# Token tile 0 of the second block first, tile 1 behind its first gathers, and float32 query products

## The chip, the cores and the metric

One core of one Trainium2 chip. The metric is the time of the whole program on the device in microseconds (us); the time of a kernel is the median of its runs. TensorE is called PE here, VectorE DVE, ScalarE ACT, GpSimd POOL and SyncE SP.

## The reference

256 tokens of 1024 channels pass two layers of a first block (three kinds of attention, an output product, a layer norm) and one layer of a second block. The change concerns the second block alone:

```python
h = rmsnorm(x, norm1_g) * (1 + sc1) + sh1
q, k, v, u = split(h @ w_in)                       # 512 channels each
attn = dilated_attention(q, k, v)                  # 8 heads of 64, causal
pool = multiscale_pool(u, pool_w, pool_scale)
x = x + g1 * (concat([attn, pool]) @ w_out)
h2 = rmsnorm(x, norm2_g) * (1 + sc2) + sh2
x = x + g2 * peer_ffn(h2, peer_wq, peer_subkeys, peer_u, peer_v)
out = rmsnorm(x, final_g)

def peer_ffn(x, w_q, sub_keys, expert_u, expert_v):    # 8 heads, q: 2 x 128 each
    s = einsum('chpk,pnk->chpn', x @ w_q, sub_keys)    # scores of 2 x 128 sub-keys
    sv, si = top_k(s, 16)                              # of each half
    top_v, top_pos = top_k(all 16 x 16 sums of sv, 16)
    eid = si[0] * 128 + si[1] at top_pos               # 16 of 16384 experts
    gate = softmax(top_v)
    act = gelu(einsum('cd,chkd->chk', x, expert_u[eid]))
    return einsum('chk,chkd->cd', gate * act, expert_v[eid])
```

## The kernel before

The tokens are two tiles of 128 (tile 0, tile 1), one token for each partition. Weights come in the order of the program through SP's queue, half a megabyte at a time (`raw`); `split` (lines 154 to 164) rounds each into a high part on ACT (`wh`, L159) and a rest on DVE (`wl`, L160), and `mm3` (L213 to L215) makes of each float32 product three quick ones: high by high, high by rest, rest by high.

**Second block** (`block2`, lines 971 to 1052). Queries and keys, values, then the pooling half are projected for both tiles. Meanwhile the dilated attention runs as a task beside the projections, piece by piece (`dilated`, `attend`): a piece is two heads of one tile, scores on PE, bias and maximum on DVE, exponentials on ACT, transposes and the product with the values on PE. The output product follows, first the pooling half of the channels, then the attention half (`y`, transposed), each for both tiles; then residual, norm (`normed`) and the transposed, scaled and shifted norm for both tiles (`affine_transposed`). `warm` puts dummy matmuls ahead of what follows.

**Experts** (`peer`, lines 1110 to 1213). For each of 8 heads the query product of both tiles (`feature`, three quick products of 128x256 for each weight tile), its copy `q`, the scores against the sub-keys (L1150) and their copy `sc`. Behind head 0 the route of (head 0, tile 0) is worked out on DVE (`route`: top 16 of each half, top 16 of their sums, the experts' numbers `eid`). The other 15 routes run later as tasks on DVE beside the rows. A route gives 16 experts for each of 128 tokens; a gather (L1165, an indirect DMA issued by POOL) brings for one of the 16 the rows `u` and `v` of all 128 tokens, 8 KB for each. That makes 16 routes x 16 = 256 gathers; the arrived tile is called a row below. DVE takes the product of `u` with the token's state, summed (L1199), ACT the gelu (L1202), DVE the gate (L1203); ACT makes a diagonal matrix `d` of the result (L1207), and PE adds `d` times `v` to the output sum in two halves of 512 channels (L1209). When PE is through with a row, its place in the buffer (`SLOTS`, 12 of 1 MB) is free for the next gather. Dot products, gelus and sums go in groups of four rows. Behind 128 rows `last` ends a tile: residual (L1174, L1175), norm, output.

Within an engine the order of the list is what the scheduler of the language makes of the program's text and of priorities; a query product stands ahead of a row's sum where its place in the text is earlier. POOL issues its gathers strictly in the order of its list.

Of the kernel before, what the change touches and what calls it, by code (L numbers as in the profile page):

```python
# [31 lines left out]
WARM = (27, 50, 25)  # L32
PACE = 0.55
SLOTS = 12
# [111 lines left out]
class Prog:  # L146
# [467 lines left out]
    def layer(self, l, x, xt, mem):  # L614
# [109 lines left out]
        for tt in range(2):  # L724
# [17 lines left out]
            if l + 1 == NL:  # L742
                self.normed(x, tt, ss[tt], self.xn)
# [186 lines left out]
    def normed(self, x, tt, ss, xn):  # L930

        nc = self.nc
        nc.vector.tensor_tensor(ss[:, 2:3], ss[:, 0:1], ss[:, 1:2], op=OP.add)
        self.rstd(ss[:, 2:3], ss[:, 2:3], 1.0 / D, self.eps6)
        self.hold = nc.vector.tensor_scalar(xn[:, tt, :512], x[:, tt, :512], ss[:, 2:3], None, op0=OP.mult)
        nc.scalar.activation(xn[:, tt, 512:], x[:, tt, 512:], AF.Copy, scale=ss[:, 2:3])

    def dilated(self, heads, qT, kT, v, y):
# [6 lines left out]
        def bias(s, ps, heads, tt):  # L945
            c = slice(128, 384) if tt else slice(0, 128)
            self.behind(nc.vector.tensor_tensor(s, ps, self.alibi[:, heads[0]:heads[1] + 1:2, c], op=OP.add))
# [23 lines left out]
    def block2(self, x, bp):  # L971
# [3 lines left out]
        self.h2 = self.xtp = bp  # L975
# [8 lines left out]
        self.alibi = bp.tile([128, 8, 384], F, name="alibi")  # L984
        qT = bp.tile([128, 4, S], F, name="q2")
        kT = bp.tile([128, 4, S], F, name="k2")
        v = bp.tile([128, 2, 512], F, name="v2")
        u = bp.tile([128, 2, 512], F, name="u2")
        y = bp.tile([128, 2, 512], F, name="y2")
# [13 lines left out]
        for h in range(8):  # L1003
            self.behind(nc.vector.scalar_tensor_tensor(self.alibi[:, h, :], dist, -float(2.0 ** -(h + 1)), lcnt, op0=OP.mult, op1=OP.add))
# [6 lines left out]
        self.pooling(u, band, wp, yp, bp)  # L1011
        g1 = self.mod[2]
        po = [[self.pacc.tile([128, 512], F, name="bank") for _ in range(2)] for _ in range(2)]

        def product(yt, first, tt, cg, j, w):
            for k in range(2):
                self.mm3(po[tt][cg], [t[:, 2 * j + k, tt * 128:(tt + 1) * 128] for t in yt],
# [260 lines left out]
```

## Time and profile before

| | us |
|---|---|
| median of 3 runs | 1453.67 (1451.47 to 1454.97) |
| the profiled execution | 1449.26 |
| its span, first to last instruction | 1447.5 |
| PE busy | 1263.4 (87%) |
| DVE busy | 1015.0 (70%) |
| ACT busy | 593.6 (41%) |
| POOL busy | 244.0 (17%) |
| all DMA | 405.30 MB, mean 280 GB/s |
| of these the gathers | 268.45 MB, 44.8% of 16 engines' span |

The profiled execution is one run, 4.4 us below the median of the three; durations are read from it alone. Shares of busy time are means over a program of very different stages, so the stages have to be read one by one. All tables of the trace count from the start of the span.

### The profile page before, as it was taken

The page shows a single profiled execution, that of the slowest core. Times are in us where ns is not written, and L with a number is a line of the kernel's source. Part 1 is how long each engine was busy: PE and PEld are TensorE (multiplying, and loading weights), DVE is VectorE, ACT ScalarE, POOL GpSimd, SP SyncE. Part 2 cuts the span into 40 slices and gives each one's busy share as a digit, 9 for nine tenths or more (in the row PEclk, how much of TensorE's full clock was granted, in tenths as well). Part 3 has the DMA queues.
Part 4 walks back from the last instruction along what each step waited for, and adds up shares of the span by engine and source line. Part 5 has one row for each costly group of instructions (what it writes and reads, how often), then busy time and mean ns, then how long its engine had stood idle before and what let it go on. Part 6 is the DMA issues. An engine that isn't in the chain of part 4 may idle for free.

```text
span 1447.5 us, 17295 instructions
## 1 busy us (share of the span) xinstructions
PE 1263.4 (87%) x5798; PEld 868.2 (60%) x5798; DVE 1015.0 (70%) x2044; ACT 593.6 (41%) x1290; POOL 244.0 (17%) x260
## 2 busy tenths in 40 slices
PE   8999999988999999989988987777787777878786
PEld 7888897767898988778777633233333332333332
DVE  6488888667589886667576677777775977755554
ACT  5567667445567665434443322222222322221112
POOL 0000000000000000000003243343333334333330
PEclk9999999999999999999998999998999899999898
DMA  8464365676563444466439799999999899999994
GB/s 303 128 221 135 115 200 168 191 222 215 168 194 98 153 146 127 166 220 200 154 115 398 300 422 421 421 422 421 421 421 422 352 421 422 421 422 421 421 421 191
DMA packets 74536, 405.30 MB, mean 280 GB/s; under 512 B 8912, under 2 KB 9296, under 8 KB 40784
## 3 DMA queue, kind: packets, MB, share of 16 engines
q0 software_dynamic: 36864, 268.45, 44.8%
q1 hardware_dynamic: 37584, 135.75, 28.5%
q8 instruction: 46, 0.75, 0.2%
q14 instruction: 42, 0.34, 0.1%
HBM read 403.12 MB, written 1.05 MB: 279 GB/s over the span
## 4 chain that ended last, share of the span: by engine, by line
PE 45%; DMA 37%; DVE 9%; ACT 4%; issue 4%; POOL 0%; DVEq 0%; ACTq 0%; POOLq 0%; SPq 0%
DMA uv<-in_puv_dram,eid 31%; PE bank L214 8%; PE bank L213 8%; PE bank L215 8%; PE acc L1209 8%; DMA raw<-in_wu_dram 6%; PE bank L371 2%; ACT wh L159 2%; DVE uv L1199 2%; DVE wl L160 2%; PE bank L461 2%; PE bank L221 1%; PE bank L510 1%; PE bank L437 1%; PE bank L549 1%
## 5 line engine op out<-in xcount | busy, mean ns | idle before, releaser
L1209 PE MATMUL acc<-uv,d 128*128 128x512 f32 x1024 | 495.2, 641 | 129.2 <-ACT d L1207 129.2
L1209 PEld LDWEIGHTS acc<-uv,d 128*128 128x128 f32 x1024 | 204.8, 205 | 414.7 <-issue 239.8
L1199 DVE CUSTOM_DVE_ANT_0 uv<-hid,uv 128x1024 f32<-128x1024 f32 x256 | 313.2, 1223 | 183.0 <-DMA uv<-in_puv_dram,eid 171.9
L1165 POOL DMA_INDIRECT uv<-in_puv_dram,eid x256 | 243.8, 952 | 1167.6 <-DVE eid L1104 761.0
L160 DVE TENSOR_TENSOR wl<-raw,wh 128x1024 fp32r<-128x1024 f32 (+1 forms) x184 | 223.2, 1214 | 122.0 <-ACT wh L159 121.6
L159 ACT ACTIVATE wh<-raw 128x1024 fp32r<-128x1024 f32 (+1 forms) x184 | 192.8, 1050 | 203.8 <-DMA raw<-in_wu_dram 92.4
L1202 ACT ACTIVATE dot<-dot 128x4 f32<-128x4 f32 (+1 forms) x66 | 13.5, 205 | 406.5 <-DVE dot L1199 406.4
L213 PE MATMUL bank<-wh,xh 128*128 128x512 f32 (+1 forms) x400 | 160.6, 403 | 1.4 <-ACT xh L258 0.8
L214 PE MATMUL bank<-wl,xh 128*128 128x512 f32 (+1 forms) x400 | 159.5, 399 | 2.2 <-DVE wl L160 2.2
L215 PE MATMUL bank<-wh,xl 128*128 128x512 f32 (+1 forms) x400 | 158.8, 398 | 0.0
L215 PE MATMUL bank<-xh,wl 128*128 128x256 f32 x384 | 110.8, 289 | 7.1 <-DVE wl L160 7.1
L213 PE MATMUL bank<-xh,wh 128*128 128x256 f32 x384 | 110.6, 288 | 4.3 <-ACT wh L159 4.3
L214 PE MATMUL bank<-xl,wh 128*128 128x256 f32 x384 | 108.0, 281 | 0.0
L1207 ACT ACTIVATE d<-ident,dot 128x128 f32<-128x128 f32 x256 | 82.9, 390 | 41.3 <-DVE dot L1203 33.6
L214 PEld LDWEIGHTS bank<-wl,xh 128*128 128x128 f32 x400 | 75.3, 188 | 18.1 <-DVE wl L160 4.0
L213 PEld LDWEIGHTS bank<-wh,xh 128*128 128x128 f32 x400 | 75.3, 188 | 17.0 <-ACT wh L159 1.1
L215 PEld LDWEIGHTS bank<-wh,xl 128*128 128x128 f32 x400 | 75.2, 188 | 15.0
L215 PEld LDWEIGHTS bank<-xh,wl 128*128 128x128 f32 x384 | 72.3, 188 | 9.4 <-DVE wl L160 8.7
L213 PEld LDWEIGHTS bank<-xh,wh 128*128 128x128 f32 x384 | 72.5, 189 | 7.8 <-ACT wh L159 5.2
L214 PEld LDWEIGHTS bank<-xl,wh 128*128 128x128 f32 x384 | 72.2, 188 | 0.5
L213 PE MATMUL bank<-nh,wh 128*128 128x256 f32 x192 | 59.5, 310 | 0.0
L214 PE MATMUL bank<-nl,wh 128*128 128x256 f32 x192 | 57.4, 299 | 1.8 <-DVE nl L259 1.5
(282 smaller groups left out, 1697.2 us busy)
## 6 DMA issues: line engine op xcount, KB each, us to landing
raw<-in_wu_dram SPq DMA_DIRECT2D x176, 512.0 KB, 4.3
raw<-in_wada_dram SPq DMA_DIRECT2D x48, 512.0 KB, 4.1
uv<-in_puv_dram,eid POOLq DMA_INDIRECT x256
raw<-in_wm_dram SPq DMA_DIRECT2D x8, 416.0 KB, 3.7
ws<-in_ws_dram SPq DMA_DIRECT2D x2, 1536.0 KB, 8.9
raw<-in_memT_dram SPq DMA_DIRECT2D x4, 512.0 KB, 4.5
lnr<-in_rows_dram SPq DMA_DIRECT2D x2, 1024.0 KB, 5.7
cb<-in_cb_dram SPq DMA_DIRECT2D x1, 1408.0 KB, 5.8
```

Source lines behind the costliest of these rows:

```text
L159: nc.scalar.activation(wh[:, :n], raw[:, :n], AF.Copy)
L160: self.last_split = nc.vector.tensor_tensor(wl[:, :n], raw[:, :n], wh[:, :n].bitcast(F), op=OP.subtract)
L213: mm(ps, a[0], b[0], start=start, stop=False)
L214: mm(ps, a[0], b[1], start=False, stop=False)
L215: self.last_mm = mm(ps, a[1], b[0], start=False, stop=stop)
L221: m = self.nc.tensor.matmul(ps, self.zero, self.zero[:, None, :].to_broadcast([128, 4, 128]), start=True, stop=True)
L371: nc.tensor.matmul(ps[:, h, k, :], st[:, c:c + 128], mv[:, c:c + 128], start=True, stop=True)
L461: nc.tensor.matmul(po[:, i, :], pt[:, i * kb + k, :], v[:, k, h * dv:(h + 1) * dv], start=k == 0, stop=k == kb - 1)
L1165: nc.gpsimd.indirect_dma_start(out=t, out_offset=None, in_=I["puv"], in_offset=bass.IndirectOffsetOnAxis(ap=eid[:, u, k:k + 1], axis=0))
L1199: self.last_split = nc.vector.tensor_tensor_reduce(out=uv[:, 0:D], in0=hid, in1=uv[:, 0:D], scale=1.0, scalar=0.0, op0=OP.mult, op1=OP.add ...
L1207: nc.scalar.activation(d, self.ident, AF.Copy, scale=dot[:, u, k:k + 1])
L1209: nc.tensor.matmul(acc[:, cg * 512:(cg + 1) * 512], d, uv[:, D + cg * 512:D + (cg + 1) * 512], start=u % 8 == 0 and k == 0, stop=u % 8 == ...
```

## The change

The second block is finished for tile 0 alone: the task beside the projections holds tile 0's attention only, and behind the pooling half's product (still of both tiles) come tile 0's attention half, residual and norm. What is left of tile 1 (attention, attention half of the output product in float32, residual, norm) is a function `rest`, which `peer` calls behind tile 0's head 0, its route, the first 8 gathers and tile 0's head 1. Heads 0 and 1 are then made for tile 1, heads 2 to 7 for both tiles. Query products are float32 (L1188: one product with unsplit operands instead of three), the transposed norm is one float32 tile `hidden`, and a state is made by transposes of it instead of products with a unit matrix. The weights of attention half and of queries come as whole tiles of 1 MB, `wo` twice, `wq` through two buffers. The 12 slots become 8, and 4 more in the memory of tile 1's work (`rows2`) from gather 24 on (`JOIN`). The first 16 rows go in groups of two (`FIRST`), and the last 25 dummy matmuls go.

```diff
-WARM = (27, 50, 25)
+WARM = (27, 50)
-SLOTS = 12
+SLOTS = (8, 4)
+JOIN = 24
+FIRST = (2, 2, 2, 2, 2, 2, 2, 2)
...
         for h in heads:
-            for tt in range(2):
-                yield from self.attend(tt, [h, h + 2], (tt + 1) * 128, score, bias, v, 64, y, [self.pps, self.pph, self.pph])
+            yield from self.attend(tt, [h, h + 2], (tt + 1) * 128, score, bias, v, 64, y, [self.pps] * 3)
...
-    def block2(self, x, bp):
+    def block2(self, x, bp, bk, hp, wq):
...
-        self.start(self.dilated((0, 1), qT, kT, v, y))
+        self.start(self.dilated((0, 1), 0, qT, kT, v, y))
         features(1)
-        self.start(self.dilated((4, 5), qT, kT, v, y))
+        self.start(self.dilated((4, 5), 0, qT, kT, v, y))
...
-        ya = self.transposed(y)
-        for j, w in halves(10):
-            for tt in range(2):
-                product(ya, False, tt, 0, j, w)
-        us = list(halves(11))
...
-        for tt in range(2):
-            residual(tt, 0)
-        for tt in range(2):
-            for j, w in us:
-                product(ya, False, tt, 1, j, w)
-            residual(tt, 1)
-            self.normed(x, tt, ss[tt], xn)
-        self.warm(WARM[2])
+        for cg in range(2):
+            nc.sync.dma_start(wo[cg], W[10 + cg])
+        self.wqs = []
+        for h in range(2):
+            self.wqs.append(wq.tile([128, 2048], F, name="wq"))
+            nc.sync.dma_start(self.wqs[h], W[12 + h])
+        for cg in range(2):
+            for j in range(2):
+                w = [t.rearrange("p (k c) -> p k c", k=2) for t in self.split(wo[cg][:, j * 1024:(j + 1) * 1024], 1024)]
+                for k in range(2):
+                    self.mm3(po[0][:, cgs[cg]], [t[:, 2 * j + k, :] for t in ya], [t[:, k, :] for t in w], False, j == 1 and k == 1)
+            residual(0, cg, ss[0])
+        hidden(0, ss[0])
+
+        def rest():
+            for heads in ((0, 1), (4, 5)):
+                for _ in self.dilated(heads, 1, qT, kT, v, y):
+                    pass
+            yt = bk.tile([128, 4, 128], F, name="yt")
+            nc.scalar.activation(yt, across(1), AF.Copy)
+            for cg in range(2):
+                for k in range(4):
+                    nc.tensor.matmul(po[1][:, cgs[cg]], yt[:, k, :], wo[cg][:, k * 512:(k + 1) * 512], start=False, stop=k == 3)
+                residual(1, cg, ss[1])
+            hidden(1, ss[1])
...
-            for h in range(8):
-                ps = self.feature(W[12 + h], ht, pb)
+            def scores(h, w, t0, nt):
+
+                n, c0 = nt * 128, t0 * 128
+                ps = self.pps.tile([128, 2, S], F, name="bank")
+                for m in range(2):
+                    for k in range(8):
+                        c = k * 256 + m * 128
+                        nc.tensor.matmul(ps[:, m, :n], w[:, c:c + 128], ht[:, k, c0:c0 + n], start=k == 0, stop=k == 7)
...
+            def gathers(done):
+
+                while len(rows) < 256 and len(rows) < done + (SLOTS[0] if len(rows) < JOIN else sum(SLOTS)):
+                    gather(len(rows))
...
+            scores(0, self.wqs[0], 0, 1)
+            hid = state(0)
+            self.finish(routing(0))
+            routes[0] = None
+            gathers(0)
+            scores(1, self.wqs[1], 0, 1)
+            acc = self.big.tile([128, D], F, name="big")
+            rest()
+            bk.release()
+            for h in range(2):
+                scores(h, self.wqs[h], 1, 1)
+            for h in range(2, 8):
+                w = wq.tile([128, 2048], F, name="wq")
+                nc.sync.dma_start(w, W[12 + h])
+                scores(h, w, 0, 2)
+            for n in range(1, 16):
+                routes[n] = routing(n)
+            pools[1] = tc.alloc_tile_pool(name="rows2", bufs=SLOTS[1], side="right")
             self.pace = PACE
-            for n in range(SLOTS):
-                gather(n)
```

On PE the last two pieces of tile 1's attention and its output product now read as follows, behind the first gather (L945 scores, L439 transposes, L463 product with the values, L1039 transposes of `y`, L1092 output product, L1273 a half row of the experts' sum):

```order
L945 MATMUL bank<-k_6042,q_6041 128x256 x2
L1273 MATMUL big<-uv,d 128x512 x4
L439 MATMUL bank<-ident,s 128x128 x4
L463 MATMUL bank<-v_6043,pt 128x64 x4
L1039 MATMUL bank<-ident,y_6045 128x128 x2
L1273 MATMUL big<-uv,d 128x512
L1039 MATMUL bank<-ident,y_6045 128x128 x2
L1273 MATMUL big<-uv,d 128x512
L1092 MATMUL big<-wo_6046,yt 128x512 x4
L1273 MATMUL big<-uv,d 128x512
L1092 MATMUL big<-wo_6047,yt 128x512 x4
L1273 MATMUL big<-uv,d 128x512 x9
```

Before, all of this stood ahead of the first head. Sums of rows stand between its steps now.

On PE the end of the query heads reads, before the change:

```order
L213 MATMUL bank<-nh_6970,wh 128x256
L214 MATMUL bank<-nl_6971,wh 128x256
L215 MATMUL bank<-nh_6970,wl 128x256
L1209 MATMUL acc<-uv,d 128x512
L1150 MATMUL bank<-sk,q 128x128 x4
L213 MATMUL bank<-nh_6948,wh 128x256
```

and now:

```order
L1194 MATMUL bank<-sk,q 128x128 x4
L1188 MATMUL bank<-hidden,wq 128x256 x16
L1273 MATMUL big<-uv,d 128x512
L1194 MATMUL bank<-sk,q 128x128 x4
L1273 MATMUL big<-uv,d 128x512 x13
L1178 MATMUL big<-ident,hidden 128x128 x7
L1273 MATMUL big<-uv,d 128x512 x472
```

One half row stands between two heads as before; tile 1's state (L1178) is made soon behind the last head and not at the change of tiles.

On POOL the gathers of the second pool (uv_7486, 7488, 7490 and 7492) stand here, behind the first 18 of the 256:

```order
L1208 DMA uv_7391<-in_puv_dram,eid_6831 128x2048
L1208 DMA uv_7412<-in_puv_dram,eid_6831 128x2048
L1208 DMA uv_7418<-in_puv_dram,eid_6831 128x2048
L1208 DMA uv_7486<-in_puv_dram,eid_6831 128x2048
L1208 DMA uv_7488<-in_puv_dram,eid_6831 128x2048
L1208 DMA uv_7434<-in_puv_dram,eid_6831 128x2048
L1208 DMA uv_7490<-in_puv_dram,eid_6831 128x2048
L1208 DMA uv_7492<-in_puv_dram,eid_6831 128x2048
L1208 DMA uv_7440<-in_puv_dram,eid_6831 128x2048
```

Gathers go in this order, so those of the first pool between them wait for the memory of tile 1's work too.

On DVE the change of tiles (residual L1174, L1175 of tile 0) reads, before:

```order
L1203 SCALAR_TENSOR_TENSOR dot<-dot,rz,gate 128x4
L1174 TENSOR_TENSOR res<-acc,macc 128x512 x2
L1175 TENSOR_TENSOR res<-res,x 128x512 x2
L1199 ISA uv,dot<-hid,uv 128x1024
L1199 ISA dot 128x1
```

and now, with dot products of tile 1 (L1263) ahead of the residual (L1222, L1223):

```order
L1263 ISA uv,dot<-big,uv 128x1024
L1263 ISA dot 128x1
L1108 MAX_INDEX si<-sv,sc 128x8
L1106 MAX sv<-sc 128x8
L1108 MAX_INDEX si<-sv,sc 128x8
L1263 ISA uv,dot<-big,uv 128x1024
L1263 ISA dot 128x1
L1222 TENSOR_TENSOR res<-big,macc 128x512 x2
L1223 TENSOR_TENSOR res<-res,x 128x512 x2
```

Four dot products of tile 1's first group have moved ahead of tile 0's residual.

## Rows read from the trace of the kernel before

**Rows 1.** Table of stretches: us, busy time of each engine, granted clock, DMA share, GB/s.

```profile
625.00:650.00 25.00, 20.91 (x115) 17.13 (x114) 15.94 (x18) 7.72 (x9) 0.00 (x0) 0.93 0.68 223
800.00:825.00 25.00, 25.00 (x143) 18.11 (x143) 16.46 (x48) 8.84 (x19) 5.62 (x6) 1.00 0.65 247
825.00:850.00 25.00, 23.05 (x51) 9.84 (x50) 18.48 (x50) 6.52 (x16) 12.04 (x13) 0.93 1.01 423
1125.00:1150.00 25.00, 19.96 (x40) 8.74 (x41) 23.36 (x68) 7.55 (x19) 8.43 (x9) 0.78 0.83 320
```

**Rows 2.** Timeline of POOL, gathers: start us, us, instruction, idle before and its releaser.

```profile
759.86 1.07 POOL L1165 DMA_INDIRECT uv<-in_puv_dram,eid  x1 [759.41 <-DVE eid L1104]
...
790.57 1.10 POOL L1165 DMA_INDIRECT uv<-in_puv_dram,eid  x1 [11.47 <-PE acc L1209]
...
807.21 0.94 POOL L1165 DMA_INDIRECT uv<-in_puv_dram,eid  x1 [7.33 <-DVE wl L160]
816.47 0.94 POOL L1165 DMA_INDIRECT uv<-in_puv_dram,eid  x1 [8.32 <-PE acc L1209]
```

**Rows 3.** Chain that ended last: start us, us, engine and line.

```profile
815.33 28.34 PE acc L1209 x66
...
1401.46 18.61 DMA uv<-in_puv_dram,eid
```

**Rows 4.** Timeline of PE, second block's output product.

```profile
714.26 1.03 PE L271 MATMUL bank<-ident,y 128*128 128x128 f32 x8
...
726.93 0.40 PE L215 MATMUL bank<-wh,xl 128*128 128x512 f32 x1
...
737.23 0.41 PE L215 MATMUL bank<-nh,wl 128*128 128x256 f32 x1
...
743.94 0.28 PE L215 MATMUL bank<-nh,wl 128*128 128x256 f32 x1
```

**Rows 5.** Timelines of PE, DVE and ACT, 654 to 670, tile 1's attention.

```profile
655.90 1.13 PE L943 MATMUL bank<-k,q 64*128 64x256 f32 x4
...
665.68 0.60 PE L437 MATMUL bank<-ident,s 128*128 128x128 f32 x4
...
667.30 1.00 PE L461 MATMUL bank<-v,pt 128*128 128x64 f32 x8
...
660.03 0.69 DVE L947 TENSOR_TENSOR s<-bank,alibi 128x512 f32<-128x512 f32 x1 [0.38 <-PE bank L437]
...
654.88 0.49 ACT L425 ACTIVATE s<-s,mx 128x256 f32<-128x256 f32 x1
```

**Rows 6.** Chain that ended last, float32 products.

```profile
356.20 6.91 PE bank L510 x32
...
813.43 0.86 PE acc L1209 x2
814.29 1.05 PE bank L1150 x8
```

**Rows 7.** Timeline of DVE, first route and first dot product.

```profile
748.26 0.49 DVE L1062 MAX8 sv<-sc 128x8 f32<-128x128 f32 x2 [1.11 <-ACT sc L1151]
...
757.57 1.22 DVE L160 TENSOR_TENSOR wl<-raw,wh 128x1024 fp32r<-128x1024 f32 x1
758.71 0.17 DVE L1104 CAST eid<-ef 128x16 uint32<-128x16 f32 x1
...
768.08 1.23 DVE L1199 CUSTOM_DVE_ANT_0 uv<-hid,uv 128x1024 f32<-128x1024 f32 x1 [9.21 <-DMA uv<-in_puv_dram,eid]
```

**Rows 8.** Timeline of ACT behind the first rows.

```profile
780.19 1.28 ACT L1202 ACT_TABLE_LOAD   x1
```

**Rows 9.** Timeline of DVE at the change of tiles.

```profile
1116.96 1.29 DVE L1174 TENSOR_TENSOR res<-acc,macc 128x512 f32<-128x512 f32 x2 [9.42 <-PE acc L1209]
```

**Rows 10.** Chain that ended last, a load of query weights.

```profile
770.48 8.04 DMA raw<-in_wu_dram
```

**Rows 11.** Page, DMA issues: count, KB each, median us from issue to landing.

```profile
raw<-in_wu_dram SPq DMA_DIRECT2D x176, 512.0 KB, 4.3
```

More of the change, by code (lines that the diff above doesn't have):

```diff
@@ L1011, in block2 @@
         self.pooling(u, band, wp, yp, bp)
+        self.pph.release()
+        self.pacc.release()
+        self.big = self.tc.alloc_tile_pool(name="big", bufs=3, space=PSUM)
+        po = [self.big.tile([128, D], F, name="big") for _ in range(2)]
         g1 = self.mod[2]
[L1013 to L1017, printed above, removed]
-                         [t[:, k, :] for t in w], first and j == 0 and k == 0, not first and j == 1 and k == 1)
+        cgs = [slice(cg * 512, (cg + 1) * 512) for cg in range(2)]
         def halves(n):
@@ new lines, in hidden @@
+        def hidden(tt, ss):
+            t = bk.tile([128, D], F, name="xn")
+            self.normed(x, tt, ss, t)
+            for j in range(2):
+                ps = self.pps.tile([128, 4, 128], F, name="bank")
+                for k in range(4):
+                    f = 4 * j + k
+                    nc.tensor.transpose(ps[:, k, :], t[:, f * 128:(f + 1) * 128], self.ident)
+                    d = self.hidden[:, f, tt * 128:(tt + 1) * 128]
+                    scale, shift = self.mod[4][:, f:f + 1], self.mod[3][:, f:f + 1]
+                    if k % 2:
+                        nc.vector.tensor_scalar(d, ps[:, k, :], scale, shift, op0=OP.mult, op1=OP.add)
+                    else:
+                        nc.scalar.activation(d, ps[:, k, :], AF.Identity, scale=scale, bias=shift)
@@ new lines, in block2 @@
+        self.hidden = hp.tile([128, 8, S], F, name="hidden")
+        ya = [bp.tile([128, 4, 128], R, name=n) for n in ("yah", "yal")]
+        ps = across(0)
+        nc.scalar.activation(ya[0], ps, AF.Copy)
+        nc.vector.tensor_tensor(ya[1], ps, ya[0].bitcast(F), op=OP.subtract)
+        ss = [self.sm.tile([128, 3], F, name="nss") for _ in range(2)]
+        for cg in range(2):
[4 more added lines that the diff above has]
+            nc.sync.dma_start(self.wqs[h], W[12 + h])
@@ L1152, in peer, with routing @@
-                if h == 0:
-                    hid = state(0)
-                    self.finish(self.start(self.route(tp, sc[:, 0, 0], iota, eid[:, 0, :], gate[:, 0, :], rz[:, 0:1])))
-            routes = [None] + [self.start(self.route(tp, sc[:, n % 8, n // 8], iota, eid[:, n, :], gate[:, n, :], rz[:, n:n + 1]))
-                               for n in range(1, 16)]
-            rows = {}
+                nc.scalar.activation(sc[:, h, t0:t0 + nt], ps[:, :nt], AF.Copy)
+            def routing(n):
+                return self.start(self.route(tp, sc[:, n % 8, n // 8], iota, eid[:, n, :], gate[:, n, :], rz[:, n:n + 1]))
@@ L1159, in gather @@
+            pools = [rp, None]
+            rows, routes = {}, {}
             def gather(n):
                 u, k = divmod(n, 16)
[L1161 to L1167 removed]
+                if routes[u] is not None:
+                    self.finish(routes[u])
+                t = pools[n >= JOIN and (n - JOIN) % sum(SLOTS) < SLOTS[1]].tile([128, 2 * D], F, name="uv")
+                nc.gpsimd.indirect_dma_start(out=t, out_offset=None, in_=I["puv"],
+                                             in_offset=bass.IndirectOffsetOnAxis(ap=eid[:, u, k:k + 1], axis=0))
+                rows[n] = t
@@ L1193, in peer @@
                     k0 = 0
-                    for size in (ENDING if u == 15 else GROUPS):
+                    for size in (FIRST if u == 0 else ENDING if u == 15 else GROUPS):
                         ks = range(k0, k0 + size)
```

167 lines of the change are left out of this document (78 added, 89 removed).

## Prediction

> **What bounds the kernel now.** I read the table of stretches first. From 825 on the 16 DMA engines are busy all the time at 421 to 423 GB/s, while DVE works 18.48 us of 25 and PE's weight loads 9.84; before that, at 625, they are not full (0.68), and between 800 and 825 they fall back to 0.65 although gathers are already running [rows 1]. So the last 620 us are the expert gathers, 256 of 1.0486 MB each (268.45 MB by the page), and at 421.5 GB/s one takes 2.488 us. Next, the queue that issues them: the first gather goes at 759.86, twelve go freely, then the queue waits for PE to finish a row and free its slot; the fifteenth goes at 807.21, and only from 816.47 on they go at the pace of PE [rows 2]. The chain of waits says why: at 815.33 PE is through with the last query head and runs 66 records of the output sum, 16.5 rows, without a pause [rows 3]. From there on nothing but bytes counts. Check: 15 gathers are issued by 815.3, 241 are left, 241 x 2.488 = 599.6, which gives 1414.9; the chain has the last one landed at 1401.46 + 18.61 = 1420.07 [rows 3], 5.2 later, of which 4.4 is the hole at 1125 (0.83 instead of 1.01 of 25 us [rows 1]). The span ends 27.4 after that landing. So
>
> span = (time PE is through with the query heads) + 2.488 x (gathers not yet issued then) + 32.6.
>
> Call that time T. Before: 815.3 + 599.6 + 32.6 = 1447.5. The whole forecast is T and the count of gathers issued by then.
>
> **The first gather.** Up to the end of the pooling half's products (714.3, from where the transposes of y follow [rows 4]) the work stands in the same order, less four pieces of attention for tile 1, plus four loads of 1 MB (two wo, two wq) hoisted into the stream of weights. The loads cost between 0 (the DMA engines have room, 0.68 at 625 [rows 1]) and 4 x 2.49 = 10 us, if each delays the half-megabyte loads behind it; the pieces give back between 0 and 11 us (PE 2.7 each: 1.13 + 0.60 + 1.00 [rows 5]). I take 0 net and keep 6 either way.
>
> From 714.3, step by step: transposes, split of y behind one weight split on ACT and DVE, 3.0; the 24 products of tile 0 instead of 48 for both, 22 of them behind the split at 0.23 a step, 5.1, to 722.4 (before: the last at 726.93 [rows 4]); residual, squares, rstd and norm as before, 4.1, to 726.5; eight transposes and eight scale-and-shift copies of 128x128 straight into one float32 tile instead of 16 with a split behind them, 1.9, to 728.4. The 25 dummy matmuls behind the last product go; nothing here waited long for them, and I count them only by the clock, next. Then the first head for tile 0: 16 float32 products of 128x128x128, two records each. The score products are the same form, eight in 1.05 at the end of a busy stretch [rows 6], 0.13 a record, so 32 x 0.14 = 4.5 at the high level of the clock. After the pause before it PE will be at the low level for a while: the products at 737.23 took 0.41, those at 743.94 0.28 [rows 4]; 1.4 more, to 734.3. Copy, four score records, copy: 1.7. The route took 748.26 to 758.88, 2.4 of it two weight splits like the one at 757.57 [rows 7]; instead it now has the bias of the first piece of tile 1's attention inside (0.69 [rows 5]) and its maximum (taken alike): 9.6. One more to the gather as before: **746.6, 13.3 earlier than before.**
>
> **From there to T.** Now the work that was ahead of the first gather stands behind it, and PE runs its list in the order shown above.
>
> - Four pieces of attention, one after the other, each a chain over three engines: scores 1.13, bias 0.69, maximum 0.69, two exponentials with their sums 1.0, transposes 0.6, copy 0.6, products with v 1.0 [rows 5], 0.6 of hand-overs: 6.3. Without the part inside the route 22.7. The third bias stands on DVE behind the dot product of the first gathered row, which landed 8.2 after its issue [rows 2, 7]; that, and table loads of 1.28 [rows 8] between exponentials and the first gelus, I put at 2.3, the low clock at 2.5: 27.5.
> - y transposed and copied with a row's half between, 2.2; the output product in float32, 16 records of 0.43 (half a row is two of them, 0.86 [rows 6]) and a half row, 7.8; residual, squares, norm with three table loads among gelus, 8.5, beside nine half rows on PE (7.7); transposes and scaling 2.2: 20.7.
> - Heads 0 and 1 for tile 1: 4.5 + 0.86 + 0.6 each: 12.
> - Six heads for both tiles: 32 records of 128x256 float32. The latent attention's query product is just this, 32 in 6.91 [rows 6]; before, a head was 48 records of 0.117 = 5.6. With one half row (0.86) and the scores (1.05 [rows 6]): 8.9 each, 53.4.
> - ACT's copy of head 5 stands behind a gelu that needs row 19, whose gather waits for a row that PE finishes behind head 4: 3.
>
> Sum 116.6, so **T = 863**. PE's own work in it, without any wait, is 100 (attention 10, output product and transposes 9, 27 half rows 23, two half heads 10, six heads 48).
>
> Gathers issued by T: PE has finished 13 rows, the eight slots give 21, and the four of the second pool stand early in POOL's list: 25, against 15 before. The gain of ten is 24.9 of DMA time, the loss of T is 47.9. One thing comes back: the hole at 1125. There the first dot products of tile 1 stood behind the final residual of tile 0, for which DVE waited 9.42 [rows 9], and behind the state that PE had still to transpose; now the state of tile 1 is built in advance and four dot products stand ahead of the residual. I take all 4.4 (between 0 and 4.4).
>
> 863.2 + 231 x 2.488 (574.7) + 28.2 = 1466.1, **18.6 over the 1447.5** of the profiled execution. That one took 1449.26, 4.4 under the median of the three runs, 1453.67; on the median I forecast **1472**. The case's own range: first gather 6 either way, the stretch to T between 107 (half of the waits hidden) and 128 (every product of the attention and a third of the heads' at the low clock): 1457 to 1490.
>
> **Rivals.** *The loads of the query weights set the pace.* Heads 2 to 7 come through two buffers of 1 MB, each load starting when the head two before it is done. Alone, half a megabyte landed in 4.3 (median), but with gathers running the one at 770.48 took 8.04 [rows 10, 11]. At 16 for a megabyte a head takes (16 + 8.9) / 2 = 12.5, six of them 21.6 more: T = 885, 1494. For it: 8.04. Against: in this stretch the gathers mostly wait for slots, so few are in flight. The Trainium skill (DMA: Bandwidth & Descriptors, Issuing engines are not separate DMA queues) says that transfers issued from different engines run on the same 16 engines and interleave, which is this rival's mechanism; the row of 8.04 agrees. Chance 0.15.
>
> *PE stays at the low level through the attention.* Its bursts of 2.7 lie between waits of 3.6; if each begins slow, as the products at 737.23 did [rows 4], and the norm's transposes too, that costs 10.8 instead of my 2.5: 1480. For it: those rows. Against: the bursts of the trace of before, which lie between other products, have 0.60 for four transposes and 1.00 for eight products, the quick level [rows 5]. Chance 0.12. By the Trainium skill (TensorE: Matmul & The Clock Gate, section HAM oscillation — how this bites in real kernels) a kernel whose bursts of products are shorter than the waits between them pays the slow clock in each burst again, which is this rival; so far the rows here show both levels.
>
> *The stream ahead of the gathers shortens.* If the four pieces leave all of their 11 and the hoisted loads cost nothing, the first gather comes at 735; with a stretch of 105 T is 840, and 840 + 574.7 + 28.2 = 1442.9, so 1449: faster. It decides at T = 844.6, where the sum equals the old span. For it: PE was busy 20.91 of 25 us at 625 [rows 1]. Against: the same stretch of weights waits mostly for its loads, which grow by 4 MB; and PE's 100 alone put T at 847 from my first gather. Chance 0.10.
>
> *The two cancel*, T near 844.6: 1453.7. Chance 0.05. That the change doesn't do what it says can be left out: the order shows the first gather ahead of tile 1's work.
>
> **The numbers.** Main case 0.58, loads 0.15, low clock 0.12, cancel 0.05, earlier stream 0.10. A difference under 0.2% (2.9 us) can't be told from none here. Faster 0.10, same 0.05, slower 0.85. Range 1456 to 1496: the main case, the low clock and the loads, without the two low ones.
>
> **What would show it.** Right: first gather near 747; between the first gather and the last head's scores some 117 us, with PE in float32 query products of about 6.9 for six heads; the DMA engines far under full between 790 and 863; 25 gathers issued by then; no hole at the change of tiles. Wrong: DMA full within 50 us of the first gather (then the slots, not PE, were never the limit), a first gather later than 753 or earlier than 740, or a stretch under 100 us, which PE's records don't allow at the high clock.

## The result, and the profile after

The changed kernel takes 1473.86 us (median of 4 runs, 1472.07 to 1475.84) against 1454.21 before: ratio 1.0139, 95% interval 1.0119 to 1.0159, 19.7 us slower. Forecast were 1472 and a range of 1456 to 1496. The profiled execution took 1472.93 with a span of 1471.2. The two profiled spans differ by 23.7 us and not by 19.7, because the profiled execution of before was 5.0 below its median.

| us from the span's start | before | forecast | after |
|---|---|---|---|
| first gather | 759.86 | 746.6 | 743.01 |
| PE through with the last query head, T | 815.33 | 863.2 | 860.75 |
| from the first gather to T | 55.5 | 116.6 | 117.7 |
| gathers issued by T | 15 | 25 | 25 |
| landing that the chain shows last (the fifth gather from the end, before and after) | 1420.07 | 1438.7 | 1443.62 |
| end of the span | 1447.5 | 1466.1 | 1471.2 |

The queue of gathers, which answers to [rows 2] (timeline of POOL, after):

```profile
743.01 1.07 POOL L1208 DMA_INDIRECT uv<-in_puv_dram,eid  x1 [742.56 <-PE bank L439]
...
767.69 0.94 POOL L1208 DMA_INDIRECT uv<-in_puv_dram,eid  x1 [14.92 <-DVE sc L1124]
...
831.73 0.94 POOL L1208 DMA_INDIRECT uv<-in_puv_dram,eid  x1 [14.21 <-PE big L1273]
851.32 0.94 POOL L1208 DMA_INDIRECT uv<-in_puv_dram,eid  x1 [18.65 <-PE big L1273]
862.04 0.94 POOL L1208 DMA_INDIRECT uv<-in_puv_dram,eid  x1 [9.79 <-PE big L1273]
```

Eight gathers go freely; from then on the gathers of the first pool wait for rows that PE finishes (only the four of the second pool, between 800 and 817, do not). Between two heads PE finishes half a row, so at the end there is one gather in 19 us. The heads themselves are the float32 products of the forecast (timeline of PE, after):

```profile
805.83 7.14 PE L1188 MATMUL bank<-hidden,wq 128*128 128x256 f32 x32 [1.06 <-DMA wq<-in_wu_dram]
812.81 1.02 PE L1273 MATMUL big<-uv,d 128*128 128x512 f32 x2
813.72 1.16 PE L1194 MATMUL bank<-sk,q 128*128 128x128 f32 x8
...
851.93 7.07 PE L1188 MATMUL bank<-hidden,wq 128*128 128x256 f32 x32
858.84 1.02 PE L1273 MATMUL big<-uv,d 128*128 128x512 f32 x2
859.75 1.16 PE L1194 MATMUL bank<-sk,q 128*128 128x128 f32 x8
860.75 11.32 PE L1273 MATMUL big<-uv,d 128*128 128x512 f32 x26
871.91 0.93 PE L1178 MATMUL big<-ident,hidden 128*128 128x128 f32 x7
878.60 21.68 PE L1273 MATMUL big<-uv,d 128*128 128x512 f32 x45 [5.76 <-ACT d L1271]
```

The table of stretches shows where the DMA engines' time went. After (compare [rows 1]):

```profile
750.00:775.00 25.00, 20.05 (x64) 11.98 (x63) 15.54 (x49) 10.89 (x26) 4.97 (x6) 0.66 0.85 337
775.00:800.00 25.00, 23.78 (x89) 12.63 (x88) 17.88 (x44) 13.03 (x30) 6.00 (x7) 1.00 0.77 293
800.00:825.00 25.00, 23.94 (x129) 20.06 (x128) 10.79 (x39) 4.54 (x11) 5.33 (x6) 1.00 0.94 360
825.00:850.00 25.00, 23.15 (x110) 19.31 (x110) 2.28 (x7) 3.17 (x7) 0.94 (x1) 1.00 0.52 199
850.00:875.00 25.00, 22.84 (x86) 14.04 (x85) 6.42 (x13) 6.07 (x10) 7.49 (x8) 1.00 0.58 211
875.00:900.00 25.00, 21.40 (x45) 9.45 (x46) 22.06 (x65) 5.16 (x17) 9.97 (x10) 0.86 0.92 363
1125.00:1150.00 25.00, 17.41 (x30) 7.01 (x29) 18.02 (x49) 9.46 (x21) 6.99 (x8) 0.78 1.01 421
```

Of the same stretches before the change, [rows 1] lacks these two and those from 850 to 900, which stood at 421 GB/s:

```profile
750.00:775.00 25.00, 20.11 (x140) 19.41 (x138) 15.41 (x43) 6.48 (x10) 10.50 (x11) 0.86 0.66 243
775.00:800.00 25.00, 21.15 (x137) 18.36 (x138) 19.65 (x45) 13.60 (x23) 3.62 (x4) 0.93 1.02 419
```

Against 421 GB/s the six stretches up to 900 lack 763 GB/s x 25 us after the change, or 45 us of DMA time. Before, the same six lack 21 (243, 419, 247, 423, 421 and 421 GB/s), half of them between 750 and 775, where the first gather has only just been issued. The hole at 1125 cost another 6.0 (320 GB/s [rows 1]) and is gone.

In full, from each kernel's first gather to the landing in the table, the profile's DMA view (the bytes moved in a window) has 270.4 MB in 660.2 us before and 274.5 MB in 700.6 us after. At 421 GB/s that leaves 17.9 and 48.5 us in which the DMA engines were idle. So the 23.7 us between the spans are 30.6 of idle time and 9.8 for the 4.1 MB more (six whole query weights are loaded behind the first gather now, six halves before), less 16.9 for the earlier first gather; behind the landing 0.2 differ. Most of the idle time lies ahead of T (table of stretches, after: attention, output product with norm, two half heads, six heads):

```profile
743.01:771.26 28.25, 20.61 (x65) 13.38 (x65) 14.87 (x43) 10.99 (x25) 9.50 (x10) 0.58 0.81 317
771.26:794.85 23.59, 22.37 (x61) 9.80 (x61) 18.02 (x46) 12.34 (x27) 6.40 (x7) 1.00 0.75 273
794.85:805.83 10.98, 9.92 (x77) 8.79 (x76) 5.36 (x12) 3.79 (x13) 3.06 (x4) 1.00 0.98 380
805.83:860.75 54.92, 53.07 (x253) 43.70 (x253) 12.76 (x42) 8.19 (x17) 4.67 (x5) 1.00 0.62 237
```

By the rates that is 7, 8, 1 and 24 us: half of all idle time is in the six heads.

Part of a difference between two profiles lies ahead of everything that was changed. The 50 dummy matmuls that end the first block begin at 601.97 before; after, the timeline of PE has them at 605.18:

```profile
605.18 11.50 PE L223 MATMUL bank<-zero 128*128 128x512 f32 x50
```

In the twelve experiments that point lies between 604.4 and 610.6 although the edits touch nothing ahead of it, so below "counted from the dummies" takes it out. What is left is still not exact: runs 5 and 12 are one program, and behind that point their profiled executions differ by 5.5 us (840.3 and 834.8). A smaller difference between two single profiles is not shown by them alone.

### The profile page after: what moved, and what is told of

Read it like the earlier page. It is cut to its first block, busy times and chain, and to the rows that moved or that the text cites. A ratio compares the mean times of both kernels' runs of the same rounds, so it can differ in the third digit from the quotient of the medians.

```text
span 1471.2 us, 16992 instructions
## 1 busy us (share of the span) xinstructions
PE 1285.4 (87%) x5685; PEld 872.2 (59%) x5685; DVE 996.3 (68%) x2039; ACT 583.9 (40%) x1285; POOL 242.6 (16%) x260
## 4 chain that ended last, share of the span: by engine, by line
PE 40%; DMA 36%; DVE 10%; issue 8%; ACT 5%; POOL 1%; DVEq 0%; POOLq 0%; ACTq 0%; SPq 0%
DMA uv<-in_puv_dram,eid 30%; PE bank L216 7%; PE bank L217 7%; PE bank L215 7%; DMA raw<-in_wu_dram 5%; PE big L1273 5%; PE bank L373 2%; DVE uv L1263 2%; DVE wl L162 2%; PE bank L463 2%; ACT wh L161 2%; POOL uv L1208 1%; PE bank L512 1%; PE bank L439 1%; PE bank L223 1%
## 5 line engine op out<-in xcount | busy, mean ns | idle before, releaser
L1273 PE MATMUL big<-uv,d 128*128 128x512 f32 x1024 | 503.9, 648 | 122.0 <-ACT d L1271 122.0
L1263 DVE CUSTOM_DVE_ANT_0 uv<-big,uv 128x1024 f32<-128x1024 f32 x256 | 313.0, 1223 | 201.3 <-DMA uv<-in_puv_dram,eid 189.4
L1273 PEld LDWEIGHTS big<-uv,d 128*128 128x128 f32 x1024 | 206.9, 208 | 408.6 <-issue 239.7
L162 DVE TENSOR_TENSOR wl<-raw,wh 128x1024 fp32r<-128x1024 f32 (+1 forms) x164 | 199.0, 1213 | 112.0 <-ACT wh L161 111.5
L161 ACT ACTIVATE wh<-raw 128x1024 fp32r<-128x1024 f32 (+1 forms) x164 | 171.8, 1050 | 173.8 <-DMA raw<-in_wu_dram 85.2
L1266 ACT ACTIVATE dot<-dot 128x4 f32<-128x4 f32 (+2 forms) x70 | 14.3, 205 | 400.0 <-DVE dot L1263 399.9
L216 PE MATMUL bank<-wl,xh 128*128 128x512 f32 (+1 forms) x384 | 152.9, 398 | 2.1 <-DVE wl L162 2.1
L215 PE MATMUL bank<-wh,xh 128*128 128x512 f32 (+1 forms) x384 | 153.9, 403 | 0.2 <-ACT wh L161 0.2
L1188 PE MATMUL bank<-hidden,wq 128*128 128x256 f32 (+1 forms) x320 | 59.6, 347 | 1.1 <-DMA wq<-in_wu_dram 1.1
L892 DVE SCALAR_TENSOR_TENSOR macc<-raw,sc,macc 128x1024 f32<-128x1024 f32 x42 | 53.7, 1279 | 6.4 <-DMA raw<-in_wada_dram 6.4
```

The costliest lines, as they stand in the source:

```text
L161: nc.scalar.activation(wh[:, :n], raw[:, :n], AF.Copy)
L162: self.last_split = nc.vector.tensor_tensor(wl[:, :n], raw[:, :n], wh[:, :n].bitcast(F), op=OP.subtract)
L215: mm(ps, a[0], b[0], start=start, stop=False)
L216: mm(ps, a[0], b[1], start=False, stop=False)
L892: self.behind(nc.vector.scalar_tensor_tensor(acc, raw, self.sc[:, k:k + 1], acc, op0=OP.mult, op1=OP.add))
L1188: nc.tensor.matmul(ps[:, m, :n], w[:, c:c + 128], ht[:, k, c0:c0 + n], start=k == 0, stop=k == 7)
```

## The experiments

The prediction's theory was: the time is set by T, because until then PE takes hardly a row and the queue stands. Its rivals were the loads of the query weights, the low clock, and a stream that shortens. A fourth came up on the way: that not T but the idle time of the DMA engines counts, of which T is only a sign.

**1. Late heads.** The product and scores of head h (2 to 7) are written at the start of the 16 rows of head h-2 instead of behind tile 1's norm, each route behind them.

```diff
-            for h in range(2, 8):
-                w = wq.tile([128, 2048], F, name="wq")
-                nc.sync.dma_start(w, W[12 + h])
-                scores(h, w, 0, 2)
...
                 for u in range(8 * tt, 8 * tt + 8):
+                    if u < 6:
+                        w = wq.tile([128, 2048], F, name="wq")
+                        nc.sync.dma_start(w, W[14 + u])
+                        scores(u + 2, w, 0, 2)
+                        routes[u + 2] = routing(u + 2)
```

> The changed kernel, with heads 2 to 7 taken out of the stretch behind the first gather: the product, scores and route of head h are written ahead of the 16 rows of head h-2, so that PE sums rows between them. Theory (the time is set by the moment PE is through with the query heads, because until then it takes no rows and the queue of gathers stands): the stretch now ends with the heads 0 and 1 of tile 1, at about 805 by the trace of the change, where 20 gathers are issued; from there the DMA engines are full, PE needs 1.72 for a row and 8.1/16 = 0.5 for the heads, under the 2.488 of a gather. Span 805 + about 4 + 236 x 2.488 + 28 = 1424, time 1420 to 1432. Rival (8 and 12 slots, not PE's list, hold the gathers back): the slots are the same, so no change, 1465 or more. Rival (heads between rows hold the routes back, and gathers wait for their route): 1435 to 1455, with DMA gaps at every 16th gather.

Measured: 1450.24 (1444.63 to 1456.24, 10 runs), ratio to before 0.9978 (0.9951 to 1.0005). 23.6 us of the change's time are back with the same slots, so their number alone was not what held the gathers; but 1424 was not reached. In the sum I had forgotten head 2, which PE's list has in one piece ahead of the rows: it ends at 822, not 805, and no gather goes for 14.8 us. The sum also left out the query weights that are loaded behind that point (4 MB by the DMA view, 10 us at 421 GB/s). The run also started its second block 5.5 us later than the changed kernel's. The time lies in the range of the rival by routes, but not its sign: from 825 to 1050 the table of stretches has 410 to 422 GB/s except once (377 between 925 and 950), and no gap at every 16th gather.

**2. Tile 1's attention back beside the projections**, everything else as in the change.

```diff
-        self.start(self.dilated((0, 1), 0, qT, kT, v, y))
+        for tt in range(2):
+            self.start(self.dilated((0, 1), tt, qT, kT, v, y))
...
-            for heads in ((0, 1), (4, 5)):
-                for _ in self.dilated(heads, 1, qT, kT, v, y):
-                    pass
             yt = bk.tile([128, 4, 128], F, name="yt")
```

> The changed kernel, with tile 1's attention back beside the projections, as before the change; tile 1's output product, norm and heads stay behind the first gathers. Theory: the attention (28.2 us from the first gather to its last product) leaves the stretch, and with it 14 of 27 half rows (12.0), while the first gather moves by 0 to 11 later; 18 gathers instead of 25 are issued by the end of the last head, 17.4 of DMA time more. Span 1471.2 - 40.2 + 17.4 + (0 to 11) = 1448 to 1459, time 1450 to 1461. Rival (the attention behind the gathers was free, the heads alone count): no change within 4, 1470 to 1478. Rival (attention beside the projections was hidden entirely): first gather unmoved at 743, time 1450.

Measured: 1480.69 (1480.29 to 1489.81, 4 runs), ratio 1.0216 (1.0163 to 1.0269): a miss. By T 18 gathers were issued, as worked out, but T came at 852.84 instead of 821 to 832. The first gather came at 765.84, 20.7 later counted from the dummies, where 11 was my upper end, and the stretch to T is 87.0 instead of 77.5. The edit was no true undoing: in the changed kernel every piece of attention takes its PSUM banks from one pool of two, which the pooling half needs too, and the pieces come in another order than before.

**7. The same with the banks of the kernel before**, two pools instead of one, and the pieces in its order.

```diff
-            yield from self.attend(tt, [h, h + 2], (tt + 1) * 128, score, bias, v, 64, y, [self.pps] * 3)
+            yield from self.attend(tt, [h, h + 2], (tt + 1) * 128, score, bias, v, 64, y, [self.pps, self.pph, self.pph])
...
         self.pooling(u, band, wp, yp, bp)
+        self.finish()
         self.pph.release()
```

> The changed kernel with tile 1's attention back beside the projections, now with the PSUM banks that the kernel before gave it (two pools instead of one pool of two banks), piece by piece in its order. Theory (in the earlier run the attention on two banks held the projections back by 20.7 us, of which the banks were half; before the change the same work took 9.9 us): first gather near 753, stretch to the last head 87 as there, 18 gathers issued by then: 840 + 592 + 7 + 28 = 1467, time 1462 to 1472. Rival (the banks do not matter, the pieces themselves hold the projections back): 1478 to 1484. Rival (attention beside the projections is free with enough banks): first gather 743, 1457.

Measured: 1467.49 (1466.95 to 1474.96, 4 runs), ratio 1.0105 (1.0060 to 1.0150). First gathers of runs 2 and 7 (timelines of POOL):

```profile
765.84 1.07 POOL L1207 DMA_INDIRECT uv<-in_puv_dram,eid  x1 [765.39 <-PE big L1091]
```

```profile
753.91 1.07 POOL L1210 DMA_INDIRECT uv<-in_puv_dram,eid  x1 [753.46 <-PE big L1094]
```

The first gather, the time and the 18 gathers came as worked out. So the four pieces beside the projections cost the first gather 9.6 us (counted from the dummies, run 7 against the changed kernel); behind the first gather they take 28 us of the stretch, in which the DMA engines move 317 GB/s of 421. Banks and order were put back together, so what each is worth stays open. By the medians that move alone made the time 6 us longer (1473.86 against 1467.49, in two series whose intervals overlap), counted from the dummies 6.7.

**3. Half the query product of heads 2 to 7**, `range(4)` for the `range(8)` blocks of channels.

```diff
-                    for k in range(8):
+                    ks = range(8) if h < 2 else range(4)
+                    for k in ks:
```

> The changed kernel, with the query products of heads 2 to 7 summed over 4 of the 8 blocks of 128 channels only: half of the product is left out, so the experts chosen by these heads are others, their number and bytes the same. Theory (PE's list sets the end of the heads): 16 records of 7.07/32 each less for six heads, 3.5 x 6 = 21 us, the order and the 25 gathers unchanged: span 1450, time 1449 to 1455. Rival (the loads of the query weights set the pace, 1 MB for each head through two buffers): a head of 5.3 us waits for its load, less than 10 us gained, 1462 to 1472. Rival (float32 heads are beside the gathers and cost nothing): 1473.

Measured: 1460.66 (1456.60 to 1462.09, 10 runs), 13.2 us under the changed kernel, where 21 was expected by one theory and under 10 by the other. In the trace the first gather comes at 747.74 and T at 849.92: the stretch is 102.2 instead of 117.7. The products gave 21, and PE waited 6.2 us for query weights (1.54, 1.43 and 3.21 ahead of three heads), against 1.06 in the changed kernel. Both mechanisms are real: PE's list is the limit at 8.8 us a head, and the loads become one at 5.4.

No run puts back the three quick products for the float32 ones. As an estimate from run 3 (20.7 us less of products for 13.2 us of time), the 1.5 us that a float32 head takes longer than a split one (7.07 against 5.6) make some 6 us over six heads. The split of the slots, the groups of two and the dropped dummies were not undone singly either.

**4. Dummy matmuls in tile 1's attention**, nine ahead of the transposes of each piece.

```diff
+            for _ in range(self.fill):
+                nc.tensor.matmul(ps.rearrange("p a b -> p (a b)"), self.zero, self.zero[:, None, :].to_broadcast([128, 4, 128]), start=True, stop=True)
```

> The changed kernel, with nine dummy matmuls ahead of the transposes of each of the four pieces of tile 1's attention, where PE waits 2.1 to 3.7 us for the exponentials at the low clock (granted 0.66 to 0.70 of the stretch). Theory: transposes 1.18 to 0.60, products with the values 1.97 to 1.0, scores 2.07 to 1.13 in three pieces, 2.5 each, 7.5 us of the stretch; the head end moves by as much: time 1464 to 1469. Rival (the pieces wait for DVE and ACT anyway, and dummies run into the transposes): no gain, 1472 to 1480.

Measured: 1473.48 (1472.14 to 1474.31, 4 runs): no gain. The clock rose (table of stretches, the changed kernel above at 0.66; with dummies):

```profile
750.00:775.00 25.00, 21.91 (x84) 14.38 (x82) 14.93 (x45) 10.73 (x26) 5.79 (x7) 0.85 0.84 343
```

but the stretch to T is 116.5 instead of 117.7. From scores to scores the first three pieces take 22.9 us instead of 25.3; the fourth, up to the transposes of `y`, takes 10.8 instead of 9.2, with 4.04 us of dummies and sums of rows between its steps. PE also still waits for the exponentials and the copies of ACT (0.3 to 1.6 us a time). So the run sets a higher clock against the time that the dummies take; what the clock alone is worth, it does not show.

**8. Rows 16 to 31 in pairs**, `FIRST` for `u < 2`.

> The changed kernel with rows 16 to 31 also in groups of two. In the changed kernel PE ran dry 11 us behind the last head for 5.76 us, because rows 20 to 23 are one group and the gathers of rows 21 to 23 were issued behind those of the second pool. Theory (this dry stretch is the 7 us by which the sum fell short behind the last head): PE takes rows 20 and 21 as soon as they land, the break shrinks to 1 to 2 us, and the time to 1468 to 1471. Rival (the ramp behind the last head is the queue's, one gather in flight at that time): no change, 1472 to 1476.

Measured: 1476.02 (1475.81 to 1476.30, 4 runs): no gain. The break in PE did shrink, from the 5.76 above (timeline of PE, run 8):

```profile
879.27 0.93 PE L1178 MATMUL big<-ident,hidden 128*128 128x128 f32 x7
881.68 8.85 PE L1273 MATMUL big<-uv,d 128*128 128x512 f32 x20 [1.48 <-ACT d L1271]
```

and from T (864.68) to the same landing (1445.08) it took 580.4 instead of 582.9. In this one profile the second block began 3.8 later, which hides a gain of 2.5; why none of the four runs is quicker is not shown.

**5 and 12. The kernel before with late heads**, its order kept.

```diff
-            for h in range(8):
-                ps = self.feature(W[12 + h], ht, pb)
...
+            for h in range(1, 2):
+                head(h)
+                routes[h] = routing(h)
...
+                    if u < 6:
+                        head(u + 2)
+                        routes[u + 2] = routing(u + 2)
```

> The kernel before the change, order of the block as it was, with heads 2 to 7 taken out of the stretch behind the first gather as in the run of the changed kernel with late heads: head h is written ahead of the rows of head h-2. Theory of the prediction (the end of the query heads, T, sets the time): T is then that of head 1, near 775, the gathers run without a break from 760, and the time falls to 1433 to 1440. Rival (from the first gather on the kernel before has hardly any idle DMA, only bytes): between the landing of the first gather (768) and of the last (1420) lie 652 us, 637 of them gathers and some 13 query weights loaded there, so that only the hole of 4.4 at the change of tiles is idle; moving the heads gains nothing, 1446 to 1454.

> The kernel before with late heads once more, as the control of the version with the early state and for its distance to the kernel before, which five runs between 1438.8 and 1448.1 had left open. Theory of the prediction (T): 14 or more below before. By idle DMA: the gap of 10 us between 800 and 825 goes and the hole of 4.8 stays, 8 to 11 below.

Measured: 1441.01 (1438.78 to 1448.06, 5 runs), ratio 0.9902 (0.9866 to 0.9937), and again 1442.02 (1441.34 to 1444.13, 7 runs), ratio 0.9938 (0.9916 to 0.9961), beside before at 1454.53 and 1452.16: 13.5 and 10.1 us below. The first run lies between the two theories, the second within the one by idle DMA. Table of stretches, run 12:

```profile
775.00:800.00 25.00, 17.98 (x92) 13.38 (x91) 16.66 (x40) 9.23 (x15) 6.53 (x7) 0.93 1.01 416
800.00:825.00 25.00, 25.00 (x123) 16.59 (x122) 20.56 (x56) 9.79 (x23) 7.98 (x8) 1.00 1.01 419
825.00:850.00 25.00, 22.59 (x113) 15.24 (x112) 19.25 (x54) 7.55 (x16) 7.49 (x8) 1.00 1.02 420
```

Where the kernel before had 247 GB/s between 800 and 825 [rows 1], now 419: 172 x 25 / 421 = 10.2 us, and counted from the dummies the span is 10.7 shorter. That the two agree so well is partly luck: the profile of run 5, the same program with 419 there too, is 5.2 shorter. The stretch in which PE takes hardly a row ended 28 us sooner (at 787.23 instead of 815.33), and the time fell by 13.5 and 10.1. By run 12 it follows the idle DMA and not T; run 5 alone, 1 us above the range by T, would not decide it.

**11. The same with tile 1's state made early**, two state tiles and one output sum in PSUM.

> The kernel before with late heads, and tile 1's state made right behind tile 0's (two state tiles and one output sum in PSUM instead of one and two). Theory (the hole at the change of tiles is DMA time lost): without it the DMA engines stay at 421 GB/s between 1125 and 1150 instead of 340, 4.8 us: 1434 to 1439 where the version with late heads alone has 1441. Rival (the wait for tile 0's residual moves to PE, which now has one output sum only, and frees slots later): no gain, 1439 to 1444.

Measured: 1442.23 (1439.36 to 1446.65, 9 runs), the same as run 12. The hole at 1125 is gone, and another has come (table of stretches, run 11):

```profile
875.00:900.00 25.00, 24.81 (x56) 10.66 (x55) 22.64 (x62) 7.21 (x19) 12.41 (x14) 0.95 0.91 359
1125.00:1150.00 25.00, 21.29 (x47) 8.99 (x46) 19.58 (x54) 5.10 (x16) 10.30 (x11) 0.94 1.02 423
```

Run 12 has 421 and 375 there (run 5 has 340 at 1125). What in the new order of PE makes the one at 875 stays open.

**6, 9 and 10. The changed kernel with late heads, better placed.** In run 6 each head's product is held behind the sum of a row by an order within PE (head 2 behind row 13, then in halves); runs 9 and 10 have in addition the first 12 or 8 rows written ahead of tile 1's output product.

```diff
+                        if behind[m] is not None:
+                            tc.add_manual_dep(mm.ins, behind[m].ins.name, NOSYNC, reason="leaves TensorE to the rows before")
```

> The changed kernel with late heads, and each product of heads 2 to 7 held behind the sum of a row by an order within PE (head 2 behind row 13, head 3's two halves behind rows 23 and 25, and so on), where the first version had head 2 in one piece ahead of them: there no gather went for 14.8 us and the DMA engines fell to 0.89 between 800 and 825. Theory (idle DMA behind the first gather is what counts): the gap of 800 to 825 and the dip at 925 to 950 go, 4 to 7 us: 1441 to 1448. Rival (only the first gather's time and the bytes count, gaps are made up later): 1448 to 1452.

> The changed kernel with late heads held behind rows, and the first 12 rows written ahead of tile 1's output product, so that PE sums them as they land and POOL gets free slots. In the run without this, gathers 9 to 16 went between 770 and 793 and the DMA engines stood at 0.73 between 775 and 800 (272 GB/s of 421: 9 us idle). Theory (idle DMA behind the first gather, not the sequence of blocks itself, is what the change costs): gathers 9 to 20 come 4 to 8 us sooner and the time falls by as much, to 1436 to 1441. Rival (the slots, 8 until tile 1's memory is free, hold the gathers back whatever PE does, and tile 1's work that is now later frees them later): 1443 to 1450.

> As the run with 12 rows ahead of tile 1's output product, with 8 rows. Theory: 1 to 2 us slower than that one, since four more rows stand behind a product, 1437 to 1443. Rival (slots): 1443 to 1450.

Measured: run 6 1444.21 (1441.84 to 1447.29, 6 runs), ratio 0.9927 (0.9903 to 0.9950), as expected by idle DMA. Run 9 1445.42 (1444.03 to 1450.29, 6 runs), ratio 0.9961 (0.9946 to 0.9975); run 10 1445.48 (1442.60 to 1448.01, 6 runs), ratio 0.9951 (0.9936 to 0.9965): no gain over run 6. Tables of stretches, run 6, then run 9:

```profile
775.00:800.00 25.00, 23.79 (x77) 11.44 (x76) 19.63 (x48) 13.46 (x30) 6.66 (x7) 1.00 0.73 272
800.00:825.00 25.00, 25.00 (x116) 17.29 (x115) 9.79 (x20) 5.25 (x16) 10.33 (x11) 1.00 0.98 396
```

```profile
775.00:800.00 25.00, 24.31 (x60) 10.68 (x58) 17.20 (x43) 8.33 (x21) 8.79 (x9) 1.00 0.98 372
800.00:825.00 25.00, 20.34 (x113) 14.69 (x113) 13.35 (x29) 10.89 (x26) 7.57 (x9) 1.00 0.94 334
```

The gathers do come sooner at first (272 to 372 GB/s), but tile 1's work is later (the last transposes of its norm end at 808.5 instead of 797.2), and then 396 falls to 334: of 100 won 62 are given back. That the slots in its memory come later is the likely reason; no run separates it from the order of PE's list.

## Why the prediction was right, and which term was off

- **First gather.** 743.01 instead of 746.6, and counted from the dummies 20.1 earlier than before instead of 13.3. The step "I take 0 net" for the stream ahead was mis-sized: the transposes of `y` begin 10.2 earlier counted from the dummies. The four pieces gave back nearly all of their 11 (9.6 by run 7), and the hoisted loads cost nothing that shows. From those transposes to the gather it took 3.5 longer than summed (35.8 against 32.3): 2.3 in the output product, which waits 1.64 for the residual between its halves, and 1.8 in the norm's transposes; the norm took 0.4 less, and head and route came as summed.
- **From the first gather to T.** 117.7 against 116.6: attention 28.3 (27.5), output product, norm and its transposes 23.6 (20.7), two half heads 11.0 (12), six heads 54.9 (53.4 and 3).
- **Gathers issued by T.** 25, as counted from the order. But the four of the second pool bring rows 24 to 27, while rows 21 to 23 were still to be issued. Their bytes are moved, but PE cannot take them yet.
- **The hole at the change of tiles** is gone, all of it: 4.4 us by the busy share that the prediction used, 6.0 by the rate.
- **Behind T.** This term was off. The sum gives 231 x 2.488 = 574.7 to the landing and 0.8 for the gaps; measured are 582.9, 8.1 more than the 574.7 (the other runs with heads in one block, 2, 3, 4, 7 and 8, have 5.7 to 8.0 more than their gathers). The 0.8 rests on a misreading: the landing at 1420.07, taken for the last, is that of the fifth gather from the end, and 3.2 MB still moved behind it, against 1.4 MB behind the landing at 1443.62. Counted to the dot product of the last row (1430.11 before, 1453.69 after), the DMA view has 253.6 and 243.0 MB behind T without the last output, and at 421 GB/s that leaves 12.5 and 15.6 us idle. So the hole's 6.0 went as forecast, but 9 came in its place. Of these, 2.6 belong to the rows for which PE ran dry (the rate falls to 8 GB/s between 883 and 884; run 8 gains 2.5 there), and some 4.6 lie at the end, where the full rate stops 9.7 us ahead of that dot product instead of 5.1. At T itself the DMA engines begin from nothing in both kernels (0 GB/s from 857 to 863, at most 16 from 813 to 818 before).
- **Sum.** The span is 1471.2 instead of 1466.1: 7.4 too little from T to the landing, 3.6 too much for the first gather, 1.1 too little for the stretch, 0.2 behind the landing. The terms partly cancel, and the sum was carried from a profile 4.4 below the median to that median, so that 1472 is nearer to 1473.86 than the sum is to its span: the nearness is partly luck, the direction and the mechanism ahead of T are not.
- **The rivals.** *Loads of the query weights*: PE waited 1.06 us for them in all of the changed kernel; run 3 shows that they bind when a head takes PE 5.4 instead of 8.8. *Low clock*: it came, with scores of 2.07 and products with the values of 1.97 in three pieces of four, and yet the attention took only 0.8 more than the main case gave it; the higher clock of run 4, dummies included, shortened the stretch by 1 us. *Earlier stream*: the first half of it came true (the pieces gave back nearly all), without the shorter stretch that it needed.
- **T as a law.** With its 32.6 the rule comes within 3.2 us where the heads stand in one block and misses by 17, 13 and 13 in runs 5, 6 and 12 (T there is the end of head 1: 789.60, 807.60 and 787.23, with 12, 18 and 12 gathers issued). It counts gathers that were issued, not bytes that have arrived: behind T these runs move 4.8 to 6.3 MB more than their remaining gathers have (260.7, 255.9 and 261.4 MB), since several gathers are in flight at T and query weights come later. What counts is the idle time of the DMA engines between the first gather and the last, 17.9 us before and 48.5 after, and the bytes that are moved there.

Both kernels are beaten by a small edit: late heads in the kernel before (1442.02 in run 12, ratio 0.9938), with its order of tiles. The change so mended (run 6) has 1444.21, beside 1441.01 for late heads in the kernel before in the same series; their ratios overlap. That holds with the heads held behind rows; with late heads placed plainly, as in the kernel before, the change has 1450.24 (run 1).

## What to carry to other kernels

When the end of a program is bound by transfers, price an earlier start of them by what keeps them fed: work that moves behind the first transfer is free only if the engine that frees the slots keeps freeing them. Look in the table of stretches for transfer rate below the full one between the first transfer and the last, since that idle time, with the bytes that move behind the first transfer, is what an edit can win or lose. Undo a part with all that it hung on (here the PSUM banks and the order of the pieces), or the run measures something else.

## What the runs showed of the hardware that was not expected

- Work that is the same in every kernel does not start at the same time: the 50 dummies began at 601.97 before, at 605.18 after and at 604.4 to 610.6 in the runs. Two single profiles have to be lined up on such a point first, and even then the same program differed by 5.5 us (runs 5 and 12).
- A higher granted clock (0.85 instead of 0.66 of a stretch, by dummies) made the attention's products with the values shorter (1.97 to 1.10, 1.11 and 1.60 in the first three pieces) and the stretch only 1 us shorter.
- At the end of the changed kernel the rate falls from 418 GB/s at 1442 to 25 GB/s, a busy share of 0.06, from 1447 to 1453, and the dot product of the last row waits for its landing until 1453.69. Before, that low stretch is 2 to 3 us long (1427 to 1430). What leaves a sixteenth of the DMA time behind is not shown.
- Between 775 and 800 run 9 has the DMA engines at 0.98 busy with 372 GB/s, run 12 at 1.01 with 416: the busy share alone does not tell the rate.
